# A hybrid conv and S5 layer on one core: the u_s stage by k tiles on unnormalised x, its result laid out anew through memory

## The chip, the cores and the metric

The kernel runs on one core of one Trainium2 chip. The metric is the device time of an execution in microseconds (us). Before the change it is 857.82 us, the median of 3 runs (857.73 to 858.01).

## The reference, cut to what matters

One decoder layer on x of 1024 positions by 1024 channels, all in float32. The input is normalised, projected by one wide matrix, and two mixers run on the projections:

```python
h = rms_norm(x, pre_g)                       # x * rsqrt(mean(x*x) + eps) * gain
proj = h @ w_in
conv_in, z_c, u_s, z_s, g_c, g_s = split(proj)
ca, cb = split(conv_in)
cu = ca * sigmoid(cb)
cu = silu(layer_norm(causal_depthwise_conv(cu, conv_w, conv_b)))     # 31 taps
conv_out = (cu * silu(z_c)) @ w_conv_out
y = gelu(s5_mimo(u_s, ...))                  # 32 groups of 16 channels, 64 complex states each
y = y * sigmoid(y @ w_glu + b_glu)
ssm_out = (y * silu(z_s)) @ w_ssm_out
merged = sigmoid(g_c) * conv_out + sigmoid(g_s) * ssm_out
return x + rms_norm(merged @ w_out, post_g)
```

The reciprocal root mean square of a position, called r below, is one number for each position: it can be multiplied in before a projection or after it. The gain is one number for each input channel.

## The kernel before, in words

**Layout.** The 1024 positions are split as 128 rows n by 8 phases t (position = 8n + t). Products are written with channels on the partitions and positions, ordered by t and then n, on the free axis. To keep float32's accuracy each operand of a matmul is split into a high and a low part (h and l), so every contraction step of 128 costs three passes: h·h, h·l and l·h. A pass of one 128-column output tile over 1024 positions is two matmuls of 512 columns. So one product with eight contraction steps (`product`, L723) has 48 matmuls.

**First stage (L759 to L821).** x comes in eight tiles by phase (`load_x`). `x_front` squares one on ScalarE with a running sum and GpSimd takes the power -1/2 of the mean; `x_mid` multiplies the tile by r and the gain on VectorE; `x_back` transposes it on TensorE in eight blocks, ScalarE copies the high part (`xh`) and VectorE subtracts to get the low part (`xl`). `us_tile` then forms u_s for this phase, 24 matmuls with x as the stationary operand, and ScalarE and VectorE copy the result into four tiles `usb` in which the eight phases of a group lie side by side. Between the passes of phase t the code places the steps of phases t+1 and t+2. The u_s weights have tiles of their own, loaded and split at the start.

**S5.** `s5_params` (L191) makes powers of the eigenvalues from a small table with many short VectorE steps, eight powers on GpSimd (L209) and three sines on ScalarE. Four calls of `s5_quarter` (L354), one for eight groups each, follow. In a quarter VectorE forms `RT`, TensorE transposes it (`rp`) and transposes `usb` (`up`, L389 to L390, 8 blocks) to get U with phase and channel on the partitions; then come the matmuls `ep` (R and U), `kp`, a chain of rotations on VectorE with sines from ScalarE, a scan, a swap of the two halves by DMA (`Zw`), two more steps, the matmuls `yp`, Gelu on ScalarE, and the transposes `yq` back. When all four are done, y is split into `yh` and `yl` (L781 to L785), which the glu products read.

**Conv branch.** `conv_gate` and `conv_taps` (L498, L509) run on VectorE, some 44 steps of 128x512 for each of eight channel tiles; then LayerNorm transposes to positions (`lnp`), takes statistics, normalises, transposes back (`lnq`), ScalarE applies silu, and VectorE multiplies by silu(z_c), read back from memory (L619). `cuh` and `cul`, the split of that, feed the eight `co` products.

**What sets the order.** The order of instructions on each engine is fixed when the program is written: instructions stand in an engine's queue in the order of the code. The products come in the list `seq` (L747 to L757): cb0, ca0, cb1, ca1, gc0 to gc7, two pairs with zc0 between, then the mark "yhl" (S5 must be done), the glu products, and so on, near the end gs6, gs7, the mark "cu", so6, so7 and co0 to co7. S5, conv and LayerNorm are generators that an emission clock (`Clock`, L628) places between the contraction steps. It works in planned units: `tick(dt)` moves the time `now` on by the planned cost of what TensorE was just given; `fg(cost)` adds VectorE work to `dve`, the time at which VectorE is reckoned free; and a generator's next step is written as soon as both its own due time and `dve` are no later than `now`:

```python
for i, t in enumerate(self.tasks):
    if max(t[1], self.dve) <= self.now:
        self.run(i)
        break
```

A step yields its VectorE cost and a delay until the next one. A contraction step of a product counts 1.296. At a mark `until` writes out all that is left of a generator at once. "cu" does so for conv and LayerNorm, "yhl" for S5.

**Buffers.** A pool of 21 tiles of 128x1024 (`T`), two buffers each for raw, high and low weights, and PSUM in two pairs of 128x1024 tiles under the tags "mm" (products) and "aux" (all else). Loads and stores are issued in order on SP; one that waits holds those behind it.

Of the kernel before, what the change touches and what calls it, by code (L numbers as in the profile page):

```python
# [11 lines left out]
ALU = mybir.AluOpType  # L12
# [23 lines left out]
def tile_hybrid_block(  # L36
    ctx: ExitStack,
    tc: tile.TileContext,
    x: bass.AP,
    w_us: bass.AP,  # L40
# [31 lines left out]
    zc_scr = nc.dram_tensor("zc_scratch", (8, 128, 1024), F32, kind="Internal").ap()  # L72
    gc_scr = nc.dram_tensor("gc_scratch", (8, 128, 1024), F32, kind="Internal").ap()
# [20 lines left out]
    iota = const.tile([128, 128], F32, name="iota")  # L94
    lamt = const.tile([128, 3, 32], F32, name="lamt")
# [4 lines left out]
    # ------------------------------------------------------------ loads  # L100
# [3 lines left out]
    xin = {}  # L104
# [5 lines left out]
    preg = T("preg")  # L110
    V.memset(mhalf, -0.5)
    V.memset(halfpi, math.pi / 2)

    # u_s weights, two k-tiles of [128, 512] in one tile
    wus, wusr = {}, {}

    def us_weights(k2):
        wusr[k2] = T(f"wusr{k2}")
        nc.sync.dma_start(out=wusr[k2], in_=w_us[k2])

    def us_split(k2):
        h, l = T(f"wush{k2}", F32R), T(f"wusl{k2}", F32R)
        A.activation(out=h, in_=wusr[k2], func=AF.Copy)
        V.tensor_tensor(out=l, in0=wusr[k2], in1=f32(h), op=ALU.subtract)
        wus[k2] = (h, l)
# [3 lines left out]
    xss = {}  # L129

    def x_front(t):
        xt = xin.pop(t)
        ssq = small.tile([128, 1], F32, tag="ssq", name=f"ssq{t}")
        A.activation(out=xl[:, :, t * 128:(t + 1) * 128], in_=xt.rearrange("p (k n) -> p k n", k=8), func=AF.Square,
                     accum_out=ssq)
        V.tensor_scalar(out=ssq, in0=ssq, scalar1=1.0 / 1024, scalar2=RMS_EPS,
                        op0=ALU.mult, op1=ALU.add)
        r = small.tile([128, 1], F32, tag="rstd", name=f"rstd{t}")
        G.tensor_tensor(out=r, in0=ssq, in1=mhalf[:, 0:1], op=ALU.pow)
        xss[t] = (xt, r)  # L140

    def x_mid(t):
        xt, r = xss[t]
        V.scalar_tensor_tensor(out=xt, in0=xt, scalar=r, in1=preg, op0=ALU.mult, op1=ALU.mult)
        clk.fg(1.2)

    def x_back(t):
        xs, _ = xss.pop(t)
        p = PS(f"xp{t}", "aux")
        for k in range(8):  # L150
            PE.transpose(p[:, k * 128:(k + 1) * 128], xs[:, k * 128:(k + 1) * 128], ident)
        pv = p.rearrange("p (k n) -> p k n", k=8)
        sl = slice(t * 128, (t + 1) * 128)
        A.activation(out=xh[:, :, sl], in_=pv, func=AF.Copy)
        V.tensor_tensor(out=xl[:, :, sl], in0=pv, in1=f32(xh[:, :, sl]), op=ALU.subtract)
        clk.fg(1.2)

    usb = {}

    def us_tile(t):  # L160
        if not usb:
            for c in range(4):
                usb[c] = T(f"usb{c}")
        p = PS(f"usp{t}", "mm")[:, 0:512]
        sl = slice(t * 128, (t + 1) * 128)
        for k in range(8):
            h, l = wus[k // 2]
            kk = slice((k % 2) * 512, (k % 2) * 512 + 512)
            PE.matmul(p, lhsT=xh[:, k, sl], rhs=h[:, kk], start=(k == 0), stop=False)  # L169
            PE.matmul(p, lhsT=xh[:, k, sl], rhs=l[:, kk], start=False, stop=False)  # L170
            PE.matmul(p, lhsT=xl[:, k, sl], rhs=h[:, kk], start=False, stop=(k == 7))  # L171
            if k == 2 and t < 7:
                x_back(t + 1)
            if k == 4 and t + 2 < 8:
                x_front(t + 2)
            if k == 6 and t + 2 < 8:
                x_mid(t + 2)
            clk.tick(0.65)
        for c in range(4):
            src = p[:, c * 128:(c + 1) * 128].rearrange("p (g h) -> p g h", g=8)  # L180
            dst = usb[c].rearrange("p (g j h) -> p g j h", g=8, j=8)[:, :, 7 - t, :]
            if c % 2:
                V.tensor_copy(dst, src)
            else:
                A.activation(out=dst, in_=src, func=AF.Copy)

    # ------------------------------------------------------------ S5
# [166 lines left out]
    def s5_quarter(c, P):  # L354
# [23 lines left out]
        # injection  # L378
# [10 lines left out]
        up = PS(f"up{c}", "aux")  # L389
        pe(lambda g, s: PE.transpose(up[:, s], usb[c][:, s], ident), 0.9)  # L390
# [22 lines left out]
        # rotation tables  # L413
# [80 lines left out]
    # ------------------------------------------------------------ conv branch  # L494
# [132 lines left out]
    # ------------------------------------------------------------ emission clock  # L627
# [41 lines left out]
    # ------------------------------------------------------------ weights  # L669
# [76 lines left out]
    # ------------------------------------------------------------ order of the products  # L746
# [12 lines left out]
    # ------------------------------------------------------------ first part: x and u_s  # L759
    load_x(0)  # L760
    nc.sync.dma_start(out=preg, in_=pre_g.partition_broadcast(128))
    us_weights(0)
    nc.sync.dma_start(out=ident, in_=ident_in)
    us_weights(1)
    load_x(1)
    us_weights(2)
    us_weights(3)
    load_x(2)
    load_x(3)
# [19 lines left out]
    x_front(0)  # L789
    x_mid(0)  # L790
    us_split(0)
    us_split(1)
    x_back(0)
    x_front(1)
    us_split(2)
    x_mid(1)
    us_split(3)
    nc.sync.dma_start(out=iota, in_=iota_in)
# [3 lines left out]
    nc.sync.dma_start(out=bmt, in_=bmat)  # L802
    nc.sync.dma_start(out=chn, in_=chan)
    nc.sync.dma_start(out=cw, in_=conv_w)
    nc.sync.dma_start(out=bgl, in_=bglu)
    clk.now = clk.dve = 0.0
    for t in range(8):
        if t == 1:
            clk.add('s5', s5_chain())
        if t == 3:  # L810
            nc.sync.dma_start(out=cmt, in_=cmat)
            nc.sync.dma_start(out=dmt, in_=dmat)
        if t == 5:
# [126 lines left out]
    # ------------------------------------------------------------ output  # L940
# [67 lines left out]
    for j in range(2):  # L1008
# [78 lines left out]
```

## Time and profile before

| | |
|---|---|
| median of 3 runs | 857.82 us |
| profiled execution, span from first to last instruction | 856.6 us |
| its own time beside the span | not listed; the median is 1.2 us above the span |
| first u_s matmul | at 11.52 us |
| first projection (`pcb`) | at 67.87 us |
| first `co` product | at 675.03 us |
| TensorE (PE) busy | 833.2 us, 97% |
| VectorE (DVE) busy | 593.7 us, 69% |
| ScalarE (ACT) busy | 300.0 us, 35% |
| granted TensorE clock, mean | 0.996 |

How to read the rows below. In a timeline a row gives the start, the duration, the engine (PE matmul, PEld weight load, DVE, ACT, POOL for GpSimd, SPq for a DMA issue), the line of the kernel, the operation, what is written from what, the shape, the count of merged instructions, and in brackets the idle time of the engine ahead of it and what ended it. In the table of stretches a row gives the stretch, its length, the busy times of PE, PEld, DVE, ACT and POOL with instruction counts, the granted clock, the busy share of the DMA engines and GB/s. In the rows of DMA issues the last number is the median time from issue to landing. In the merged chain of work a row gives start, length and what was run.

### The profile page before, as it was taken

How to read it: one execution, taken by the hardware profiler on the slowest of the kernel's cores; microseconds unless marked ns; L12 is line 12 of the kernel's file. 1: busy time of each engine (PE TensorE's matmuls, PEld its weight loads, DVE VectorE, ACT ScalarE, POOL GpSimd, SP SyncE). 2: the span in 40 equal slices, each digit the busy share in tenths (PEclk: the TensorE clock that was granted, in tenths of full speed). 3: DMA queues.
4: the chain of work that ended last, by engine and by line, in shares of the span. 5: the costliest groups of instructions: out<-in, count | busy, mean ns of one | idle time of the engine just before them, and what ended most of it. 6: DMA issues, size and time to landing. Idle time of an engine off the chain costs nothing.

```text
span 856.6 us, 9977 instructions
## 1 busy us (share of the span) xinstructions
PE 833.2 (97%) x3968; PEld 691.3 (81%) x3968; DVE 593.7 (69%) x861; ACT 300.0 (35%) x373; POOL 33.6 (4%) x40
## 2 busy tenths in 40 slices
PE   5999999999999999999999999999999999999996
PEld 4778888888888878888888888788788888888885
DVE  5587898898979999898998999422234744452242
ACT  5333534444435451333322131245644511122121
POOL 0600000000000000000000000010000000000010
PEclk9999999999999999999999999999999999999999
DMA  9202303414323021111121232111216543325142
GB/s 330 104 1 75 84 30 83 138 64 137 99 73 77 26 85 51 50 50 50 37 86 39 74 123 95 54 72 66 72 62 230 221 146 141 143 91 196 50 172 99
DMA packets 28559, 82.93 MB, mean 97 GB/s; under 512 B 7440, under 2 KB 7824, under 8 KB 28512
## 3 DMA queue, kind: packets, MB, share of 16 engines
q1 hardware_dynamic: 28512, 82.29, 28.4%
q8 instruction: 31, 0.51, 0.2%
q14 instruction: 16, 0.13, 0.0%
HBM read 60.13 MB, written 16.78 MB: 90 GB/s over the span
## 4 chain that ended last, share of the span: by engine, by line
PE 92%; DVE 3%; ACT 2%; issue 2%; DMA 1%; SPq 0%; POOL 0%; DVEq 0%; ACTq 0%; POOLq 0%
PE pgc L731 10%; PE pca L731 10%; PE pcb L731 10%; PE pco L731 10%; PE pzc L731 10%; PE po L961 10%; PE pgs L731 9%; PE pzs L731 5%; PE pso L731 5%; PE pgl L731 2%; PE usp L171 1%; PE usp L169 1%; PE usp L170 1%; PE lnq L584 1%; PE yp L482 1%
## 5 line engine op out<-in xcount | busy, mean ns | idle before, releaser
L529 DVE SCALAR_TENSOR_TENSOR pp<-ext,cw,pp 128x512 f32<-128x512 f32 x232 | 165.3, 744 | 1.6 <-ACT pp L520 1.6
L529 DVE SCALAR_TENSOR_TENSOR acc<-ext,hs,acc 128x512 f32<-128x512 f32 x120 | 89.2, 744 | 0.0
L961 PE MATMUL po<-wox,mgh 128*128 128x512 f32 x192 | 52.3, 389 | 0.0
L961 PEld LDWEIGHTS po<-wox,mgh 128*128 128x128 f32 x192 | 36.0, 188 | 7.5
L731 PE MATMUL pzc<-xh,wh_zc 128*128 128x512 f32 x128 | 40.7, 400 | 0.0
L731 PE MATMUL pgc<-xh,wh_gc 128*128 128x512 f32 x128 | 40.3, 396 | 0.0
L731 PE MATMUL pgs<-xh,wh_gs 128*128 128x512 f32 x128 | 40.1, 394 | 0.0
L731 PE MATMUL pca<-xh,wh_ca 128*128 128x512 f32 x128 | 40.0, 394 | 0.0
L731 PE MATMUL pzc<-xl,wh_zc 128*128 128x512 f32 x128 | 40.0, 394 | 0.0
L731 PE MATMUL pcb<-xh,wh_cb 128*128 128x512 f32 x128 | 39.9, 393 | 0.0
L731 PE MATMUL pzc<-xh,wl_zc 128*128 128x512 f32 x128 | 39.8, 393 | 0.0
L731 PE MATMUL pcb<-xh,wl_cb 128*128 128x512 f32 x128 | 39.5, 390 | 0.0
L731 PE MATMUL pgs<-xl,wh_gs 128*128 128x512 f32 x128 | 39.4, 389 | 0.0
L731 PE MATMUL pgc<-xl,wh_gc 128*128 128x512 f32 x128 | 39.4, 389 | 0.0
L731 PE MATMUL pgs<-xh,wl_gs 128*128 128x512 f32 x128 | 39.4, 389 | 0.0
L731 PE MATMUL pco<-cuh,wh_co 128*128 128x512 f32 x128 | 39.4, 389 | 0.0
L731 PE MATMUL pco<-cuh,wl_co 128*128 128x512 f32 x128 | 39.4, 389 | 0.0
L731 PE MATMUL pca<-xl,wh_ca 128*128 128x512 f32 x128 | 39.4, 389 | 0.0
L731 PE MATMUL pgc<-xh,wl_gc 128*128 128x512 f32 x128 | 39.4, 389 | 0.0
L731 PE MATMUL pcb<-xl,wh_cb 128*128 128x512 f32 x128 | 39.4, 389 | 0.0
L731 PE MATMUL pca<-xh,wl_ca 128*128 128x512 f32 x128 | 39.4, 389 | 0.0
L731 PE MATMUL pco<-cul,wh_co 128*128 128x512 f32 x128 | 39.4, 389 | 0.0
(260 smaller groups left out, 1765.6 us busy)
## 6 DMA issues: line engine op xcount, KB each, us to landing
xin<-in_x_dram SPq DMA_DIRECT2D x8, 512.0 KB, 4.7
wr_cb<-in_w_in_dram SPq DMA_DIRECT2D x8, 512.0 KB, 3.3
wr_ca<-in_w_in_dram SPq DMA_DIRECT2D x8, 512.0 KB, 3.2
wr_gc<-in_w_in_dram SPq DMA_DIRECT2D x8, 512.0 KB, 3.4
gc_scratch<-gct SPq DMA_DIRECT2D x8, 512.0 KB, 2.8
wr_zc<-in_w_in_dram SPq DMA_DIRECT2D x8, 512.0 KB, 3.3
zc_scratch<-zct SPq DMA_DIRECT2D x8, 512.0 KB, 2.6
wr_gs<-in_w_in_dram SPq DMA_DIRECT2D x8, 512.0 KB, 3.2
```

The source lines that it names most:

```text
L169: PE.matmul(p, lhsT=xh[:, k, sl], rhs=h[:, kk], start=(k == 0), stop=False)
L170: PE.matmul(p, lhsT=xh[:, k, sl], rhs=l[:, kk], start=False, stop=False)
L171: PE.matmul(p, lhsT=xl[:, k, sl], rhs=h[:, kk], start=False, stop=(k == 7))
L482: PE.matmul(yp[:, s], lhsT=Sx[:, s], rhs=O1[:, s], start=False, stop=True)
L529: V.scalar_tensor_tensor(out=o, in0=src(e, r), scalar=w, in1=o, op0=ALU.mult, op1=ALU.add)
L584: PE.transpose(q[:, s], tn[:, s], ident)
L731: PE.matmul(p[:, js(j)], lhsT=lhs[:, ks], rhs=rhs(k, j), start=st, stop=sp_)
L961: PE.matmul(p[:, js(j)], lhsT=lhs[k][:, s], rhs=rhs[k][:, js(j)], start=st, stop=sp_)
```

## The change

x is also given transposed, as `xt` of eight tiles by channel (128 channels by 1024 positions in the order t, n). The first stage no longer waits for r: it runs over the eight contraction tiles k, with all four u_s output tiles accumulating in the eight PSUM banks ("aux" and "mm" both), weights as the stationary operand. x is scaled by the gain alone and split (`x_raw`). The squares still come from x by phase; when all eight are done, r is formed at once for all (`x_rstd`), written to memory as 8 by 128, and read back as one row on all partitions (`rbc`). The u_s results are multiplied by it as they leave PSUM (`us_out`), stored to `us_scr`, and read back in eight pieces, one for each phase, directly as U. The transposes `up` of the S5 quarters and the tiles `usb` go. The projections after the stage still need normalised x, so `x_norm` multiplies each raw tile by gain and r and splits it again into `xh` and `xl`. The u_s weights now share the two raw, high and low weight buffers. `seq` and the generators' costs stay, but for the clock calls of the new stage and the `up` group's 0.9.

```diff
+    us_scr = nc.dram_tensor("us_scratch", (4, 128, 1024), F32, kind="Internal").ap()
+    r_scr = nc.dram_tensor("r_scratch", (8, 128), F32, kind="Internal").ap()
...
+    def us_split(k2, part, parts):
...
+        A.activation(out=h[:, s], in_=wusr[k2][:, s], func=AF.Copy)
+        V.tensor_tensor(out=l[:, s], in0=wusr[k2][:, s], in1=f32(h[:, s]), op=ALU.subtract)
+        clk.fg(1.15 / parts)
...
+    def x_raw(k):
+        A.activation(out=xh[:, k, :], in_=xraw[k], func=AF.Copy, scale=gcol[:, k:k + 1])
+        V.scalar_tensor_tensor(out=xl[:, k, :], in0=xraw[k], scalar=gcol[:, k:k + 1], in1=f32(xh[:, k, :]),
+                               op0=ALU.mult, op1=ALU.subtract)
+        clk.fg(1.28)
+
+    def x_square(t):
+        xi = xin.pop(t)
+        A.activation(out=xi, in_=xi, func=AF.Square, accum_out=ssq8[:, t:t + 1])
+
+    def x_rstd():
+        V.tensor_scalar(out=ssq8, in0=ssq8, scalar1=1.0 / 1024, scalar2=RMS_EPS, op0=ALU.mult, op1=ALU.add)
+        G.tensor_tensor(out=r8t, in0=ssq8, in1=mhalf, op=ALU.pow)
+        nc.sync.dma_start(out=r_scr.rearrange("t n -> n t"), in_=r8t)
+        rbc = T("rbc")
+        nc.sync.dma_start(out=rbc, in_=r_scr.rearrange("t n -> (t n)").partition_broadcast(128))
+        return rbc
+
+    def x_norm(k, rbc):
+        xn = xraw.pop(k)
+        V.scalar_tensor_tensor(out=xn, in0=xn, scalar=gcol[:, k:k + 1], in1=rbc, op0=ALU.mult, op1=ALU.mult)
+        A.activation(out=xh[:, k, :], in_=xn, func=AF.Copy)
+        V.tensor_tensor(out=xl[:, k, :], in0=xn, in1=f32(xh[:, k, :]), op=ALU.subtract)
+        clk.fg(2.5)
...
+    def us_out(m, p, rbc):
+        u = T(f"usT{m}")
+        V.tensor_tensor(out=u, in0=p, in1=rbc, op=ALU.mult)
         clk.fg(1.2)
+        nc.sync.dma_start(out=us_scr[m], in_=u)
+        usU[m] = T(f"U{m}")
+        src = us_scr[m].rearrange("(g h) (t n) -> t h g n", g=8, t=8)
+        for t in range(8):
+            nc.sync.dma_start(out=usU[m][16 * (7 - t):16 * (8 - t)].rearrange("p (g n) -> p g n", g=8), in_=src[t])
...
-        up = PS(f"up{c}", "aux")
-        pe(lambda g, s: PE.transpose(up[:, s], usb[c][:, s], ident), 0.9)
...
-        U = T(f"U{c}")
-        A.activation(out=U, in_=up, func=AF.Copy)
+        U = usU[c]
...
+    load_xt(0)
+    nc.sync.dma_start(out=gcol, in_=pre_g)
+    us_weights(0, 2)
+    load_xt(1)
     load_x(0)
...
+    usp = {m: PS(f"usp{m}", "aux" if m < 2 else "mm") for m in (0, 1, 2, 3)}
+    for k in range(2):
+        x_raw(k)
+        us_split(0, k, 2)
+    rbc = None
+    for k in range(8):
...
+        if k + 2 < 8:
+            x_raw(k + 2)
+            if k % 2 == 0:
+                us_split(k // 2 + 1, 0, 1)
+        for t in {0: (0,), 1: (1, 2), 2: (3, 4), 3: (5, 6), 4: (7,)}.get(k, ()):
+            x_square(t)
+        if k == 4:
+            rbc = x_rstd()
             for _ in range(WRAW):
                 wload()
...
+        ms = (2, 3, 0, 1)
+        runs = [(m, i) for m in ms for i in range(3)] if k == 7 else [(m, i) for i in range(3) for m in ms]
+        for n_, (m, i) in enumerate(runs):
...
+            if n_ == 5:
+                for k_ in {5: (0, 1, 2), 6: (3, 4), 7: (5,)}.get(k, ()):
+                    x_norm(k_, rbc)
+            if k == 6 and n_ == 8:
+                wsplit_h()
+                wsplit_l()
+            clk.tick(0.45)
+            if k == 7 and i == 2:
+                if m == 0:
+                    x_norm(6, rbc)
+                us_out(m, usp[m], rbc)
+    x_norm(7, rbc)
```

In the loop the S5 generator is added at k = 1 (at t = 1 before). The loads of x, xt, the u_s weights and the small tables are issued in a new order, among and ahead of these steps.

More of the change, by code (lines that the diff above doesn't have):

```diff
@@ L39, in tile_hybrid_block @@
     x: bass.AP,
+    xt: bass.AP,
     w_us: bass.AP,
@@ L102, in tile_hybrid_block @@
     ov = out.rearrange("(n t) d -> t n d", t=8)
-    xin = {}
+    V.memset(mhalf, -0.5)
+    V.memset(halfpi, math.pi / 2)
+    xin, xraw = {}, {}
     def load_x(t):
@@ L108, in load_x, with load_xt, us_weights @@
         nc.sync.dma_start(out=xin[t], in_=xv[t])
-    preg = T("preg")
-    V.memset(mhalf, -0.5)
-    V.memset(halfpi, math.pi / 2)
+    def load_xt(k):
+        xraw[k] = T(f"xt{k}")
+        nc.sync.dma_start(out=xraw[k], in_=xt[k])
     wus, wusr = {}, {}
[L117 to L125, printed above, removed]
+    def us_weights(k2, parts=1):
+        wusr[k2] = wp.tile([128, 1024], F32, tag="wraw", name=f"wusr{k2}", bufs=WRAW)
+        n = 1024 // parts
+        for i in range(parts):
+            nc.sync.dma_start(out=wusr[k2][:, i * n:(i + 1) * n], in_=w_us[k2][:, i * n:(i + 1) * n])
@@ new lines, in us_split @@
+    def us_split(k2, part, parts):
+        if part == 0:
+            wus[k2] = (wp.tile([128, 1024], F32R, tag="wh", name=f"wush{k2}", bufs=WHL),
+                       wp.tile([128, 1024], F32R, tag="wl", name=f"wusl{k2}", bufs=WHL))
+        h, l = wus[k2]
+        n = 1024 // parts
+        s = slice(part * n, (part + 1) * n)
+        A.activation(out=h[:, s], in_=wusr[k2][:, s], func=AF.Copy)
+        V.tensor_tensor(out=l[:, s], in0=wusr[k2][:, s], in1=f32(h[:, s]), op=ALU.subtract)
+        clk.fg(1.15 / parts)
@@ L142, in x_mid @@
-    def x_mid(t):
-        xt, r = xss[t]
-        V.scalar_tensor_tensor(out=xt, in0=xt, scalar=r, in1=preg, op0=ALU.mult, op1=ALU.mult)
-        clk.fg(1.2)
[L147 to L185, printed above, removed]
+    ssq8 = const.tile([128, 8], F32, name="ssq8")
@@ L757, in tile_hybrid_block @@
     order += [u for u in seq if u[0] not in NOW] + [("wo", k) for k in range(WHL)]
+    load_xt(0)
+    nc.sync.dma_start(out=gcol, in_=pre_g)
+    us_weights(0, 2)
+    load_xt(1)
     load_x(0)
-    nc.sync.dma_start(out=preg, in_=pre_g.partition_broadcast(128))
-    us_weights(0)
-    nc.sync.dma_start(out=ident, in_=ident_in)
+    load_xt(2)
     us_weights(1)
[L765 to L769, printed above, removed]
     nc.sync.dma_start(out=lamt, in_=lam)
     nc.sync.dma_start(out=cst, in_=cst_in)
+    load_x(1)
+    load_x(2)
+    load_xt(3)
+    load_x(3)
+    load_xt(4)
     P5 = {}
@@ new lines, in tile_hybrid_block @@
+    for k in range(2):
[3 more added lines that the diff above has]
+    for k in range(8):
+        if k == 0:
+            load_x(4)
+            us_weights(2)
+            load_x(5)
+            load_x(6)
+            load_xt(5)
+            load_x(7)
+            nc.sync.dma_start(out=bmt, in_=bmat)
+        if k == 1:
+            clk.add('s5', s5_chain())
+            nc.sync.dma_start(out=chn, in_=chan)
+            nc.sync.dma_start(out=cw, in_=conv_w)
+            load_xt(6)
+        if k == 2:
+            us_weights(3)
+            load_xt(7)
+            for d_, s_ in ((iota, iota_in), (ident, ident_in), (bgl, bglu), (cmt, cmat), (dmt, dmat)):
+                nc.sync.dma_start(out=d_, in_=s_)
+        if k + 2 < 8:
[6 more added lines that the diff above has]
+            rbc = x_rstd()
@@ new lines, in tile_hybrid_block @@
+        for n_, (m, i) in enumerate(runs):
+            lhs, rhs = passes[i]
+            for j in range(2):
+                js_ = slice(j * 512, (j + 1) * 512)
+                PE.matmul(usp[m][:, js_], lhsT=lhs[:, kk[m]], rhs=rhs[:, k, js_], start=(k == 0 and i == 0),
+                          stop=(k == 7 and i == 2))
+            if n_ == 5:
[9 more added lines that the diff above has]
+                us_out(m, usp[m], rbc)
```

49 lines of the change are left out of this document (10 added, 39 removed).

## The prediction

> **What bounds the kernel now.** I read the page first: the span, the engines, the chain of work that ended last.
>
> ```profile
> span 856.6 us, 9977 instructions
> PE 833.2 (97%) x3968; PEld 691.3 (81%) x3968; DVE 593.7 (69%) x861; ACT 300.0 (35%) x373; POOL 33.6 (4%) x40
> PE 92%; DVE 3%; ACT 2%; issue 2%; DMA 1%; SPq 0%; POOL 0%; DVEq 0%; ACTq 0%; POOLq 0%
> ```
>
> TensorE is the bound. Next the busy times by stretch, cut at the first projection (67.87), the first glu product (294.06) and the first co product (675.03).
>
> ```profile
> 67.87:294.06 226.19, 226.19 (x1234) 191.73 (x1233) 199.24 (x270) 100.49 (x101) 3.82 (x4) 1.00 0.29 84
> 294.06:675.03 380.97, 376.85 (x1713) 311.08 (x1712) 277.06 (x402) 138.43 (x185) 7.85 (x8) 1.00 0.22 77
> 675.03:856.60 181.57, 174.54 (x769) 143.93 (x767) 73.16 (x71) 32.59 (x42) 4.40 (x8) 0.99 0.39 139
> ```
>
> Per stretch: length, then PE, PEld, DVE, ACT, POOL. From 67.87 to 675.03 TensorE idles 0.00 + 4.12 us: every chain on VectorE ends just in time, by an order of instructions that is fixed in advance. VectorE is busy 88% of the first stretch. So two questions decide: does the first projection start sooner than 67.87, and do the chains still end in time? What lies after 675.03 is the same work in both; I keep its 181.6.
>
> **The first stage, TensorE's side.** The timeline and the merged chain:
>
> ```profile
> 4.21 1.06 ACT L134 ACTIVATE xl<-xin 128x1024 fp32r<-128x1024 f32 x1 [2.20 <-DMA xin<-in_x_dram]
> ...
> 11.52 0.80 PE L169 MATMUL usp<-wush,xh 128*128 128x512 f32 x1 [1.36 <-ACT xh L154]
> ...
> 14.03 0.63 PE L170 MATMUL usp<-wusl,xh 128*128 128x512 f32 x1
> ...
> 14.45 0.63 PE L171 MATMUL usp<-wush,xl 128*128 128x512 f32 x1
> ...
> 75.71 0.87 PE up L390 x8
> ...
> 95.62 10.88 PE pcb L731 x48
> ```
>
> Warm, a 512-column matmul takes a slot of 10.88/48 = 0.227 us; early on the slot is 0.42 (14.03 to 14.45). The first raw transposed tile should land as the first x tile does (4.2); scaling it (1.06), half a weight split and the gain's small load put the first matmul at about 6.5 instead of 11.5. The 192 matmuls take 43.5, slow slots at first add some 2: u_s ends near 52. If that were all, the first projection would start 16 us sooner. The four `up` groups, 0.87 each, go as well: **-3.5**.
>
> **The first stage, VectorE's side.** The projections need normalised x, and it comes from one queue: eight x_norm, each a VectorE multiply, a ScalarE copy that VectorE waits for, and a VectorE subtract, with the us_out between them. The steps, from equal operations:
>
> ```profile
> 6.62 1.28 DVE L144 SCALAR_TENSOR_TENSOR xin<-xin,rstd,preg 128x1024 f32<-128x1024 f32 x1 [1.07 <-DMA preg<-in_pre_g_dram]
> ...
> 7.91 1.06 ACT L123 ACTIVATE wush<-wusr 128x1024 fp32r<-128x1024 f32 x1 [2.55 <-DMA wusr<-in_w_us_dram]
> ...
> 9.00 1.23 DVE L124 TENSOR_TENSOR wusl<-wusr,wush 128x1024 fp32r<-128x1024 f32 x1 [1.09 <-ACT wush L123]
> ...
> 22.86 3.26 POOL L209 TENSOR_TENSOR spt<-ebase,lamt 128x8 f32<-128x8 f32 x2 [2.28 <-DVE ebase L203]
> 38.88 0.18 DVE L212 SCALAR_TENSOR_TENSOR spt<-spt,spt 128x32 f32<-128x32 f32 x1
> ...
> 41.04 0.19 DVE L199 TENSOR_TENSOR turns<-turns,spt 128x32 f32<-128x32 f32 x1
> 0.00:22.00 22.00, 12.16 (x46) 9.41 (x46) 11.40 (x15) 10.84 (x14) 1.86 (x7) 1.00 0.90 332
> preg<-in_pre_g_dram SPq DMA_DIRECT2D x1, 512.0 KB, 5.3
> bgl<-in_bglu_dram SPq DMA_DIRECT2D x1, 2.0 KB, 3.7
> wr_cb<-in_w_in_dram SPq DMA_DIRECT2D x8, 512.0 KB, 3.3
> gc_scratch<-gct SPq DMA_DIRECT2D x8, 512.0 KB, 2.8
> ```
>
> One x_norm is 1.28 + 1.09 + 1.23 = 3.6, since nothing stands between its two VectorE steps; a us_out or a weight's subtract is 1.2. When can the first begin? It needs all eight squares, the power, r to memory and back.
>
> The loads do not set this: at 332 GB/s (row of 0 to 22) the 10.6 MB up to the last u_s weight land by 32. What does is the S5 parameters' order on VectorE. Raw tile 3 is the ninth 512 KB: 4.7 MB at 332 is 14, its copy and subtract end at 17.4, and only then comes the memset that S5's first powers wait for. Four powers of 1.63 on GpSimd (3.26 for two) end at 24, 0.7 of VectorE, four more at 31.4. The steps on theta stand in VectorE's queue ahead of raw tile 6, and there it waits: 2.7 for them (the same steps ran from 38.9 to 41.2), tile 6 and weight split 3 (2.5), the small step: 36.8. A power on 128x8 is 1.64: 38.5.
>
> The round trip of r is not in the trace. Its store is 1,024 pieces of 4 bytes. From below it is a 2 KB load (3.7 beside other loads; without them perhaps 2.4) and a plain 512 KB load (3.3), so 5.7; from above I double the first and take the broadcast row, 7.4 + 5.3 = 12.7. I take 3.7 + 5.3 = 9.0, the rows of like shape. So the row of r is there at **47.5** (44 to 51).
>
> The Trainium skill, "DMA: Bandwidth & Descriptors", "Rules for kernel authors", speaks against this store: a strided last dimension becomes one descriptor per element. No run here shows its price; by that page's fit for the GpSimd path (2.0 us plus bytes/436 GB/s, "Anatomy of one DMA") an estimate for both trips is 5.2, and the sum below would be 3.8 less.
>
> From 47.5, in VectorE's order: x_norm 0 to 4 (18.0), cb0's weight subtract, us_out 2, which frees the PSUM pair that cb0 writes: 47.5 + 18.0 + 2.4 = 67.9. **cb0 starts where it starts now**, after TensorE has idled some 16 us. Then x_norm 5, us_out 3, x_norm 6, us_out 0 and 1, x_norm 7: 10.8 + 3.6 = 14.4, to 82.3. cb0's last contraction step, due 9.5 after its start, at 77.4, needs that: **+4.9** (+1.5 to +8.5).
>
> SP's queue: each us_out is a store (2.8 and its issue) and eight loads that wait for it, issued at about 0.6 as the eight `Mt` copies are (254.93, in the next fence: 5.24 for x8): 8 us, four times, from 67.9 to 100. Behind them is the load of ca1's weights, landing at 103, split at 105.5, when ca1 begins (83.7 + 2 x 10.9): 0 (to +6). U of quarter 0, third in that order, lands near 94; its first reader stands at 112.
>
> **The order written ahead.** Products and VectorE tasks are placed by the emission clock; I followed its costs through both listings. Before: the stage ends at 41.6 of the clock, VectorE reckoned free at 39.9. After: 96 ticks of 0.45 are 43.2, but 8 x 2.5 + 4 x 1.2 + 1.14 from 29.3 on make VectorE free at 55.2. So the rest of S5's parameters waits, and quarter 0 starts 26 units into the projections instead of 1. Before, S5's last step comes at 257.06 and the place where glu needs it ("yhl") at 257.06: no slack. After, "yhl" stands at 250.7, with quarter 3's kp product emitted at 239.8, seven contraction steps earlier. All that is left of S5 is then put there in one piece, with no product between. The trace has each step:
>
> ```profile
> 249.33 0.21 PE L424 MATMUL kp<-O,bb 128*16 128x16 f32 x2
> ...
> 252.41 0.28 DVE L438 TENSOR_TENSOR kr<-kp,dmt 16x128 f32<-16x128 f32 x1 [4.34 <-ACT kr L437]
> ...
> 254.93 5.24 SPq L445 DMA_DIRECT2D Mt<-kr  x8
> ...
> 256.74 0.74 DVE L529 SCALAR_TENSOR_TENSOR pp<-ext,cw,pp 128x512 f32<-128x512 f32 x1
> ...
> 257.40 0.74 DVE L529 SCALAR_TENSOR_TENSOR acc<-ext,hs,acc 128x512 f32<-128x512 f32 x1
> ...
> 268.01 2.63 DVE L463 TENSOR_TENSOR_SCAN Zs<-r,Et 128x128 f32<-128x128 f32 x8
> ...
> 275.44 1.23 DVE L371 TENSOR_TENSOR Zw<-Zw,tk 128x1024 f32<-128x1024 f32 x1 [0.89 <-DMA Zw<-Zs]
> ...
> 285.23 1.28 ACT L486 ACT_TABLE_LOAD   x1 [5.31 <-PE yp L482]
> ...
> 286.52 1.03 ACT L486 ACTIVATE yt<-yp 128x1024 f32<-128x1024 f32 x1
> ...
> 289.09 1.03 PE L489 MATMUL yq<-ident,yt 128*128 128x128 f32 x8
> ...
> 292.21 4.63 DVE L784 TENSOR_TENSOR yl<-y,yh 128x1024 fp32r<-128x1024 f32 x4 [1.41 <-ACT yh L783]
> ```
>
> From kp's start: kr at 3.1, its 0.28 and five S5 steps (0.7 + 4 x 1.2), six conv taps (0.66 each) and one half weight (0.7) queued between: 13.4; the add 1.2; scan to 17.1; half swap (270.64 to 275.44) to 21.9; two more steps: 24.4. TensorE is there after 1.8 + 7 x 1.36 = 11.4: it waits 13.0 for yp. Then yp 3.5, Gelu and its table load 2.5, yq, and from yq's start 7.75 until the fourth split (289.09 to 296.84): glu's last step at 38.2, its end at 39.1, against 21.2 without waits: **+17.8** (+14 to +20).
>
> LayerNorm likewise. The last conv channel ends at 519.4 of the clock instead of 495.5, "cu" stands at 599.4 (603.2). Before, all eight rounds and all multiplies by z were placed by 603.2; after, round 8 and the eight multiplies fall behind "cu", with only so6 and so7 as cover.
>
> ```profile
> 545.84 1.03 PE L559 MATMUL lnp<-ident,acc 128*128 128x128 f32 x8
> ...
> 551.73 1.09 PE L584 MATMUL lnq<-ident,tn 128*128 128x128 f32 x8 [2.12 <-ACT tn L575]
> ...
> 645.41 2.90 ACT L588 ACTIVATE acc<-lnq,chn 128x128 f32<-128x128 f32 x8
> ...
> 650.43 2.35 DVE L619 TENSOR_TENSOR acc<-acc,zcr 128x1024 f32<-128x1024 f32 x2
> ...
> 666.00 1.23 DVE L619 TENSOR_TENSOR acc<-acc,zcr 128x1024 f32<-128x1024 f32 x1 [2.09 <-DMA zcr<-zc_scratch]
> ```
>
> lnp to lnq is 5.9 here, with a first power of 1.5; 5.1 with the usual 0.55, less 0.8 of its own: 4.3. From lnq: silu 1.3 to 4.2, eight multiplies 9.8 if back to back, 16.8 as they run now (650.43 to 667.2, waiting for loads); I take 12.8: 17. so7's weights are subtracted behind them (0.7), while so7 wants its third pass at 0.8 + 5.5 + 0.9 = 7.2: 10.5. Together **+14.8** (+11 to +19). co0 finds its splits in time. Of the 4.1 idle now, lnq0's 2.1 stays: **-2.0**.
>
> After long idle TensorE is slow, as at the start: 3.2 us at 0.42 are 7.5 matmuls, 0.2 each, 1.5. At "yhl" and "cu" together **+3.0**; from below 0, if a wait inside the kernel leaves no trace, from above 4. The Trainium skill, "TensorE: Matmul & The Clock Gate", Part 1, says that the array falls to half its clock after an idle window of about 3.4 us. The slow slots at 14 agree with that, though the granted clock reads 1.00 in that stretch; no long idle time later on is in this trace to show it.
>
> Sum: -3.5 + 4.9 + 0 + 17.8 + 14.8 - 2.0 + 3.0 = **+35.0**. Span 891.6. The median, 857.82, is 1.2 above the profiled span: **893**.
>
> **The rivals.** *The clock's lag is not real and the row of r is early* (chance 0.08): if x_norm keeps up with TensorE the projections start at 52 and S5 has time; 857.8 - 16 - 3.5 = 838. For it: VectorE has 12% to spare. Against: it decides only if the row of r is there by 52 - 20.4 = 32, and the queue gives 38.5 before the round trip. *Only the first stage counts* (0.04): +4.9 - 3.5, 859; it needs "yhl" and "cu" covered, and no product stands there. *Half cover* (0.12): r early and the multiplies back to back, with one of the waits at "yhl" or "cu" gone: 893 - 16 = 877. *SP's queue decides* (0.10): the 32 U loads keep weights from ScalarE through several products, as ScalarE stands still behind each; twice 6 us: 905. Forecast: 0.66.
>
> **How the numbers follow.** All lows of the terms give 878, all highs 911; both at once are unlikely. With the half-cover case below and the queue's above the range is 874 to 906; it leaves out the first two rivals and the forecast's own tails, some 2 in 10. A difference under 0.2% (1.7 us) I call the same: the runs shown spread 0.3 us. Faster: 0.08. Same: most of the 859 case, 0.03. Slower: the rest, 0.89.
>
> **What would show it.** Right: TensorE idle from about 52 to 68, waiting for us_out 2; x_norm steps 3.6 apart, the first waiting for rbc's load; a wait of 13 before yp in the last quarter, right ahead of glu; a wait at the last lnq and one in so7. Wrong: cb0 starting by 60, an uninterrupted TensorE around glu, or the eighth lnp well ahead of so6.

## The result and the profile after

The changed kernel takes **948.0 us** (median of 4 runs, 947.43 to 949.99) against 857.81 us (4 runs, 857.73 to 858.01): a ratio of 1.1057, 95% interval 1.1041 to 1.1073. It is slower, as forecast, but by 90 us instead of 35, and outside the range. The page of the changed kernel (profiled in the run of 949.99), its span and the busy times of the engines:

```profile
span 948.0 us, 9816 instructions
PE 843.0 (89%) x3872; PEld 696.2 (73%) x3872; DVE 605.3 (64%) x851; ACT 304.1 (32%) x364; POOL 28.8 (3%) x33
```

TensorE had 97% and has 89%: it waits. VectorE's busy time grew by 11.6 us only, so the change does not cost work, it costs waiting. The table of stretches of the changed kernel, cut where the prediction cut it: at the first projection (74.75), the first glu product (323.06) and the first `co` product (766.55). Columns: length, then busy times of PE, PEld, DVE, ACT, POOL, then granted clock, DMA share, GB/s.

```profile
74.75:323.06 248.31, 230.66 (x1201) 193.34 (x1201) 209.36 (x300) 96.39 (x95) 3.82 (x4) 0.96 0.32 93
323.06:766.55 443.49, 392.39 (x1713) 321.77 (x1713) 287.42 (x414) 144.41 (x190) 5.94 (x8) 0.93 0.20 69
766.55:948.00 181.45, 174.54 (x769) 143.88 (x767) 72.78 (x71) 32.30 (x41) 4.32 (x8) 0.99 0.38 133
```

The last stretch is what it was (181.45 against 181.57). The first projection comes 6.9 later, the next stretch is 22 longer, and the one from glu to `co` is 62.5 longer: the larger part of the loss lies nearly 300 us behind the edited stage, at the waits from 380 on. Which waits? The table of TensorE's waits (sum, times, longest), cut:

```profile
PE pcb L724 <- DVE usT L175: 22.0, 1, 22.0
PE pso L724 <- ACT wh_so L691: 19.9, 2, 10.6
PE pzs L724 <- ACT wh_zs L691: 16.0, 2, 9.7
PE yp L475 <- DVE Sx L468: 12.2, 1, 12.2
PE lnq L577 <- ACT tn L568: 8.1, 4, 4.0
...
PE pso L724 <- DVE wl_so L699: 6.5, 1, 6.5
...
```

The rows for `usT`, `Sx`, `tn` and the `wl_so` row are the prediction's own waits. The rows for `wh_so` and `wh_zs`, 35.9 us in four waits, stand nowhere in it. The timeline around the first of these four, in the changed kernel:

```profile
360.42 1.23 DVE L699 TENSOR_TENSOR wl_zs<-wr_zs,wh_zs 128x1024 fp32r<-128x1024 f32 x1 [5.40 <-ACT wh_zs L691]
361.56 0.75 DVE L522 SCALAR_TENSOR_TENSOR pp<-ext,cw,pp 128x512 f32<-128x512 f32 x1
...
381.64 0.68 DVE L532 TENSOR_TENSOR acc<-acc,pp 128x512 f32<-128x512 f32 x1
...
382.28 1.18 DVE L494 TENSOR_TENSOR ext<-pca,sg 128x1024 f32<-128x1024 f32 x1
383.50 0.71 DVE L497 TENSOR_TENSOR ext<-ext 128x528 f32<-128x528 f32 x1
384.24 1.19 ACT L498 ACTIVATE ext<-ext 128x1179 f32<-128x1179 f32 x1 [23.85 <-DVE ext L497]
385.33 1.04 ACT L691 ACTIVATE wh_zs<-wr_zs 128x1024 fp32r<-128x1024 f32 x1
...
386.43 1.22 PE L724 MATMUL pzs<-xh,wh_zs 128*128 128x512 f32 x2 [6.28 <-ACT wh_zs L691]
```

Read it upwards from the last row. TensorE waits for a high weight half on ScalarE. That copy takes 1.04 and its data is there, but ScalarE, which works in order, has stood for 23.85 behind the gate's copy into `ext` (L498). That copy waits for the gate on VectorE, and the gate stands behind the whole rest of the last convolution channel, 361.56 to 382.3, without a break. This is the line `clk.until('conv', lambda: conv_left[0] < n)`: if two channels are pending when a gate comes, the rest of one is written ahead of it in one piece. The emission clock does this at gates 4, 5, 6 and 7 after the change, with 15 to 20 of its units in each piece, and at none before. In the trace ScalarE stands behind these four gates for 23.9, 27.3, 27.4 and 28.6 us.

How long each stretch has become, in the changed kernel (start and end, then length): the two pairs of `zs`, the first `gs` with its `so`, `gs` 1 with `so` 1, the last S5 quarter with glu, and the stretch at cu.

```profile
369.10:398.97 29.87, 23.59 (x97) 19.05 (x96) 19.88 (x29) 6.45 (x6) 0.00 (x0) 0.89 0.10 36
420.73:455.42 34.69, 24.94 (x98) 20.04 (x96) 23.29 (x34) 6.44 (x6) 0.00 (x0) 0.80 0.09 31
477.18:505.38 28.20, 18.81 (x74) 15.06 (x72) 20.46 (x32) 3.82 (x5) 0.00 (x0) 0.82 0.12 38
527.14:556.56 29.42, 18.86 (x74) 15.06 (x72) 21.63 (x34) 3.82 (x5) 0.00 (x0) 0.83 0.09 27
299.92:347.34 47.42, 31.44 (x137) 26.29 (x136) 22.33 (x29) 14.56 (x16) 0.00 (x0) 0.82 0.14 41
737.42:766.55 29.13, 18.67 (x66) 14.85 (x64) 19.71 (x21) 17.45 (x25) 0.54 (x1) 0.71 0.52 184
```

Without waits a projection takes 10.88 and an `so`, or a glu product, half of that. So the first four cost 29.87 - 21.76 = 8.1, 12.9, 28.20 - 16.32 = 11.9 and 13.1: **46.0** together. The fifth holds yp, yq and four glu products, 3.5 + 0.85 + 21.76 = 26.1 without waits: **+21.3**. The sixth holds `so` 6, `so` 7 and one lnp and lnq, 12.6: **+16.5**. At the start cb0 ends at 90.33 instead of 78.75: **+11.6**. With the four `up` groups gone (-3.5) the sum is 91.9; `co` 0 starts 91.5 later. Not all of this is waiting: in these rows TensorE is also busy longer than the work takes, by 10.0 at the four gates together, 5.3 in the fifth and 6.1 in the sixth. That is the slow clock after a wait, shown in the last section.

The first stage of the changed kernel, its timeline:

```profile
37.65 1.64 POOL L158 TENSOR_TENSOR r8t<-ssq,mhalf 128x8 f32<-128x8 f32 x1 [4.88 <-DVE spt L229]
39.31 0.40 SPq L159 DMA_DIRECT2D r_scratch<-r8t  x1
48.33 0.34 SPq L161 DMA_DIRECT2D rbc<-r_scratch  x1
54.48 1.28 DVE L166 SCALAR_TENSOR_TENSOR xt<-xt,gcol,rbc 128x1024 f32<-128x1024 f32 x1 [11.33 <-DMA rbc<-r_scratch]
...
74.75 1.19 PE L724 MATMUL pcb<-xh,wh_cb 128*128 128x512 f32 x2 [22.02 <-DVE usT L175]
```

The load of r's row waits for its store, issued 9.0 earlier; from the store's issue to the first x_norm pass 15.2.

### The profile page after: what moved, and what is told of

Same layout as the page of the kernel before. It is cut to its first block, busy times and chain, and to the rows that moved or that the text cites. A ratio compares the mean times of both kernels' runs of the same rounds, so it can differ in the third digit from the quotient of the medians.

```text
span 948.0 us, 9816 instructions
## 1 busy us (share of the span) xinstructions
PE 843.0 (89%) x3872; PEld 696.2 (73%) x3872; DVE 605.3 (64%) x851; ACT 304.1 (32%) x364; POOL 28.8 (3%) x33
## 2 busy tenths in 40 slices
DMA packets 36221, 91.31 MB, mean 96 GB/s; under 512 B 9344, under 2 KB 13824, under 8 KB 36176
## 3 DMA queue, kind: packets, MB, share of 16 engines
q1 hardware_dynamic: 36176, 90.69, 28.6%
## 4 chain that ended last, share of the span: by engine, by line
PE 58%; DVE 24%; ACT 5%; DMA 5%; issue 5%; POOL 2%; SPq 1%; DVEq 0%; POOLq 0%; ACTq 0%
PE pzc L724 9%; PE pco L724 9%; PE po L985 9%; DVE pp L522 8%; PE pcb L724 6%; PE pgs L724 5%; PE pso L724 5%; DVE acc L522 4%; PE pca L724 3%; PE pzs L724 3%; PE pgl L724 2%; PE pgc L724 2%; DMA xt<-in_xt_dram 1%; POOL spt L205 1%; DMA Zw<-Zs 1%
## 5 line engine op out<-in xcount | busy, mean ns | idle before, releaser
L522 DVE SCALAR_TENSOR_TENSOR pp<-ext,cw,pp 128x512 f32<-128x512 f32 x232 | 164.6, 744 | 12.7 <-ACT pp L513 12.7
L498 ACT ACTIVATE ext<-ext 128x1179 f32<-128x1179 f32 x8 | 9.5, 1186 | 138.3 <-DVE ext L497 138.3
L724 PEld LDWEIGHTS pcb<-xh,wh_cb 128*128 128x128 f32 x128 | 24.1, 192 | 28.7 <-issue 22.6
L724 PE MATMUL pso<-y2h,wh_so 128*128 128x512 f32 x64 | 24.0, 461 | 19.9 <-ACT wh_so L691 19.9
```

The costliest lines, as they stand in the source:

```text
L498: A.activation(out=ext[:, :, 0:3, 1:132], in_=ext[:, :, 4:7, 0:131], func=AF.Copy)
L522: V.scalar_tensor_tensor(out=o, in0=src(e, r), scalar=w, in1=o, op0=ALU.mult, op1=ALU.add)
L724: PE.matmul(p[:, js(j)], lhsT=lhs[:, ks], rhs=rhs(k, j), start=st, stop=sp_)
```

## The experiments

The theory: the loss is in the order that the emission clock writes. Its lag makes it put pieces ahead of gates, of yp and behind cu, and the engines that work in order then hold weights back. The main rival: VectorE really has too little time, wherever the pieces stand. A separate question is r's round trip. Each experiment is one run, only the last has six; the kernel before took 856.3 to 858.7 us beside them. The six runs of the last version spread over 2.9 us, so a smaller difference between single runs isn't read as a gain.

**The clock set back at the end of the stage.** Only the written order of what follows differs.

```diff
     P5_ready[0] = True
+    clk.dve = clk.now
```

> The new kernel with one line more: at the end of the first stage the emission clock's reckoning of VectorE is set back to its present time (55.2 to 43.2). No work is added or removed, only the places of later instructions move. Theory (written order: S5 and conv are placed too late against the products, and what is left at the marks and ahead of gates 4 to 7 is written in one piece that holds back the next weights): the four pieces ahead of the gates shrink from 15 to 20 units to 5 to 10, so the four waits (46 us over the matmuls' own time with the slow slots after them) fall to 10 to 15, the one at glu (21) to about 10, the end (16.5) to about 11; 890 to 905. Rival (the new stage's extra VectorE work, its memory traffic and SP's queue are the cost): 944 to 950, as the work is the same.

Measured: 919.87. The gain, 28, is outside both bands. TensorE's waits in this run:

```profile
PE pca L724 <- DVE wl_ca L699: 8.3, 2, 7.5
...
PE pso L724 <- ACT wh_so L691: 4.8, 2, 2.6
PE yp L475 <- DVE Sx L468: 4.6, 1, 4.6
PE pzs L724 <- ACT wh_zs L691: 2.8, 1, 2.8
```

The gates' waits fall from 35.9 to 7.6 and yp's from 12.2 to 4.6, with VectorE's work unchanged. But the clock now calls VectorE free when it isn't: the rest of the S5 parameters is written ahead of ca0's low half, and TensorE waits 7.5 there. The wait in `so` 7 stayed at 6.5. The order is the cause, but pretending that the lag is gone is no cure.

**r stored as 128 by 8**, and read by VectorE in steps of 32 bytes.

```diff
-        nc.sync.dma_start(out=r_scr.rearrange("t n -> n t"), in_=r8t)
+        nc.sync.dma_start(out=r_scr, in_=r8t)
...
+        return rbc.rearrange("p (n t) -> p t n", t=8)
```

> The new kernel, but r goes to memory as 128 rows of 8 (128 pieces of 32 bytes, as it lies) instead of 8 rows of 128 (1,024 pieces of 4 bytes); the broadcast row is then read by VectorE with a stride of 8. Theory (the many small pieces of the store are the dear half of r's round trip of 15 us): the store lands in 2.5 to 3.5 instead of 8.6, the first x_norm starts at 48 to 49 instead of 54.5, the first projection near 69 instead of 74.75, and the time falls by 5 to 6: 942. Rival (what costs is the two trips' fixed latency, not the pieces): the store still takes over 6, 946 to 949. If the strided read slows VectorE, x_norm's first step shows it (1.28 now).

Measured: 947.58. The timeline of this run:

```profile
38.66 0.35 SPq L159 DMA_DIRECT2D r_scratch<-r8t  x1
40.10 0.33 SPq L161 DMA_DIRECT2D rbc<-r_scratch  x1
44.25 2.18 DVE L167 SCALAR_TENSOR_TENSOR xt<-xt,gcol,rbc 128x1024 f32<-128x1024 f32 x1 [1.75 <-DMA rbc<-r_scratch]
```

The store lets the load go after 1.4 instead of 9.0, and the first x_norm runs 10.2 earlier. But every x_norm multiply, which reads the row, takes 2.05 to 2.20 instead of 1.28, and VectorE's queue gives the gain back: cb0 starts at 69.42, 5.3 earlier, then waits 5.8 for the last x_norm and ends at 90.49 (90.33 in the change). The time alone would have said that the store doesn't matter; the trace says that it does and that the edit paid for it elsewhere.

**A row of ones instead of r**: no store, no load, and so no normalisation of x.

```diff
-        nc.sync.dma_start(out=r_scr.rearrange("t n -> n t"), in_=r8t)
         rbc = T("rbc")
-        nc.sync.dma_start(out=rbc, in_=r_scr.rearrange("t n -> (t n)").partition_broadcast(128))
+        G.memset(rbc, 1.0)
```

> The new kernel without r's trip through memory: the row that x_norm and us_out multiply by is filled with ones on GpSimd, so the normalisation is left out and nothing waits for the squares. Theory (r's round trip is what x_norm waits for, all of it on the path to the first projection): x_norm starts when VectorE has finished raw tile 7, near 43.5, the first projection stands near 64 instead of 74.75, and the total falls by 10 to 11: 937. Rival (the stage is bound by VectorE's own queue or by TensorE): the first projection moves by less than 4, 944 or more.

Measured: 937.01, as the theory had it. TensorE's wait at cb0:

```profile
PE pcb L723 <- DVE usT L174: 10.0, 1, 10.0
```

It is 12 shorter (22.0), the time 11; the waits at the gates, at yp and in `so` 7 are the same to 0.1. So the whole round trip is worth 11 us of the 90, and an earlier start moves nothing of the rest: there the order decides.

**The gate's copy on GpSimd** instead of ScalarE, so that ScalarE no longer stands behind the gate.

```diff
-        A.activation(out=ext[:, :, 0:3, 1:132], in_=ext[:, :, 4:7, 0:131], func=AF.Copy)
+        G.tensor_copy(ext[:, :, 0:3, 1:132], ext[:, :, 4:7, 0:131])
```

> The new kernel, with the copy at the end of each conv gate on GpSimd instead of ScalarE, so that ScalarE's queue doesn't stand behind VectorE there. Theory (VectorE's own piece ahead of the gate holds the low half of the next weights as well, which stands behind the gate in its queue): each of the four waits shrinks by 1 to 3 only, 936 to 946. Rival (it is ScalarE's standing, with the high halves behind it, that stops TensorE): the four waits go, and with them 36 to 46: 902 to 912.

Measured: 937.56. TensorE's waits in this run:

```profile
PE pso L724 <- DVE wl_so L699: 19.8, 3, 7.9
...
PE pzs L724 <- DVE wl_zs L699: 9.3, 2, 6.3
```

The waits for high halves are gone, and waits for low halves stand in their place: VectorE's own queue has the piece ahead of those too. (The longest of the first row, 7.9, is `so` 7's. At the four gates 21.2 are left for low halves and 5.4 for PSUM tiles that ScalarE empties, of 35.9.) ScalarE's standing behind the gate was the last wait to end, and worth about 10 us; the piece on VectorE is the cause.

**The order alone.** The first stage stays as in the change. First LayerNorm's delays, then the place of three products, then both (with one product more moved, ahead of cb6 and ca6).

```diff
-        yield 0.0, 3.0
+        yield 0.0, 2.0
...
-        yield 1.4, 2.2
+        yield 1.4, 2.0
...
-        yield 0.1, 5.4
+        yield 0.1, 3.0
```

> Edit: the changed kernel with LayerNorm's three delays on the emission clock alone made shorter (3.0, 2.2, 5.4 become 2.0, 2.0, 3.0); the list of products is as in the change. On the clock the multiplies by z then end 2 behind cu instead of 25 behind it. Theory (the excess at cu, 16.5, comes from where those steps are written): the waits at the last lnq and in so7 go, those at the gates and at yp stay as they are: 931 to 936. Rival (VectorE reaches these steps late whatever their place): above 943.

Measured: 935.60. The waits at the gates and at yp are 19.9, 16.0 and 12.2 as before; the wait in `so` 7 is gone, and the longest at lnq is 2.8. Of the 16.5 at cu, some 12 went by three numbers of the clock.

```diff
-    seq = pairs[0] + pairs[1] + gc + pairs[2] + zc[0:1] + pairs[3] + [("yhl", 0)] + glu + pairs[4] + zs[0:2]
+    seq = pairs[0] + pairs[1] + gc + pairs[2] + zc[0:1] + pairs[3] + zc[1:4] + [("yhl", 0)] + glu + pairs[4] + zs[0:2]
-    seq += pairs[5] + zs[2:4] + pairs[6] + [("y2", 0)] + gso[0] + pairs[7] + gso[1] + gso[2] + zc[1:8]
+    seq += pairs[5] + zs[2:4] + pairs[6] + [("y2", 0)] + gso[0] + pairs[7] + gso[1] + gso[2] + zc[4:8]
```

> Edit: the changed kernel with three zc products alone moved ahead of glu; LayerNorm's delays are as in the change. On the clock no piece stands ahead of gates 4 to 7, nothing is left of S5 at yhl, and the multiplies by z end 15 behind cu instead of 25. Theory (46.0 at the gates and 21.3 at yp come from the place of these products): both go but for a few us, and of the 16.5 at cu some 7 to 12 stay: 881 to 892. Rival (the moved products bring the waits of the gates back at other places): above 900.

Measured: 877.26, better than the band by 4. TensorE's waits behind cb0 are these and two of 0.7 and 0.2:

```profile
PE lnq L577 <- ACT tn L568: 6.8, 3, 2.8
PE pso L724 <- DVE wl_so L699: 4.7, 1, 4.7
PE pgl L724 <- DVE wl_glu L699: 1.8, 1, 1.8
```

No wait at a gate or at yp is left, and `so` 7's is shorter: 70.7 us from the place of three products, with no work added or removed.

> Edit: the first stage as in the changed kernel; only the list of products is other (three zc products stand ahead of glu, one ahead of the sixth pair) and LayerNorm's three delays on the emission clock are shorter (3.0, 2.2, 5.4 become 2.0, 2.0, 3.0). By the clock's arithmetic no piece is then put ahead of a gate, before yp or behind cu without cover. Theory (46.0 at the gates, 21.3 at yp and 16.5 at the last lnq and so7 come from the written order alone): the first projection starts as before at 74.8, those waits shrink to some 2 to 3 each, and the time is 866 to 885. Rival (VectorE's work does not fit behind the products since it begins them later, wherever the pieces are put): the waits come back elsewhere and the time stays above 915.

Measured: 870.71. The table of stretches of this run, from its first projection to glu and from glu to `co`:

```profile
74.79:337.08 262.29, 260.01 (x1344) 217.69 (x1345) 232.83 (x330) 108.12 (x106) 3.83 (x4) 0.99 0.33 97
337.08:687.03 349.95, 343.76 (x1570) 284.34 (x1569) 263.54 (x385) 129.02 (x176) 6.48 (x8) 1.00 0.22 76
```

The first projection comes where it came, at 74.8; behind it TensorE idles 2.3 + 6.2 us instead of 17.7 + 51.1. VectorE's busy time in the two, 496.4, is what it was (209.36 + 287.42 = 496.8). The rival is refuted: VectorE had time enough for the same work.

**The start of the projections.** Both edits build on r stored as 128 by 8. First ScalarE brings the row into the order of t once, so that VectorE's steps are contiguous again; then VectorE issues the next multiply ahead of the last low half.

```diff
+        rb = T("rb")
+        A.activation(out=rb.rearrange("p (t n) -> p t n", t=8), in_=rbc.rearrange("p (n t) -> p t n", t=8), func=AF.Copy)
+        return rb
...
```

> Edit: r is stored as 128 pieces of 32 bytes, and ScalarE brings the broadcast row into the order of t once (1.1 us), so that VectorE reads it contiguously again. Theory (the round trip of r delays the start of the projections one for one, and nothing behind it gives the time back): the first x_norm at about 46 instead of 54.5, the first projection about 20.3 behind it at 66 instead of 74.8, the time some 8.5 below the changed kernel: 938 to 941. Rival (VectorE's lag at the waits further on decides, wherever the projections start): 945 to 949.

Measured: 945.16, a miss, and by the time alone the rival's. The trace shows that the step expected, an earlier x_norm, did not come about. The timeline of this run:

```profile
44.34 2.15 ACT L163 ACTIVATE rb<-rbc 128x1024 f32<-128x1024 f32 x1 [10.31 <-DMA rbc<-r_scratch]
...
48.40 1.13 ACT L147 ACTIVATE xh<-xt,gcol 128x1024 fp32r<-128x1024 f32 x1
49.57 1.28 DVE L148 SCALAR_TENSOR_TENSOR xl<-xt,gcol,xh 128x1024 fp32r<-128x1024 f32 x1 [10.18 <-ACT xh L147]
```

The copy stands in ScalarE's queue ahead of raw tile 7, so ScalarE waits 10.3 for the row, tile 7 is late, and VectorE's queue has tile 7's low half ahead of the first x_norm, which runs at 52.0 and not at 46.

```diff
+        xnq.append((k, xn))
+        if len(xnq) > 1:
+            x_low()
...
```

> Edit: the one before, and VectorE issues the multiply of the next x_norm before the low part of the last one, so that it doesn't stand waiting for ScalarE's copy. Theory: x_norm about 2.5 apart instead of 3.6; five of them stand ahead of the first projection, so it starts some 5.5 sooner, near 61; the waits at the gates, at yp and in so7 stay, since their order is the same: 930 to 936. Rival (ScalarE's copy becomes the step that sets the pace): no more than 2 below the run before.

Measured: 938.23, outside the band, since the run that it builds on was 4 us worse than expected; the step itself brought 6.9. x_norm runs 2.3 apart instead of 3.55.

**Both together**, then two repairs of the stage: the copy of the row behind raw tile 7, and r formed earlier.

> Edit: the runs with the pipelined x_norm and with the other order together. Theory (the start of the projections and the order add up): 14 below the run with the other order alone, 850 to 870, and near 852 if its waits are as small as the clock says, which is below the kernel before. Rival (with TensorE waiting less, another engine's chain ends last, so that the two don't add): less than 6 below the run with the other order alone.

Measured: 862.04, inside the band, but 8.7 below the run with the other order alone and not 14. The same edits of the start had brought 9.8 without the other order (948.0 to 938.23): but for 1.1 they add up, and the start itself is worth less than expected, since the copy is misplaced.

```diff
-        rb = T("rb")
-        A.activation(out=rb.rearrange("p (t n) -> p t n", t=8), in_=rbc.rearrange("p (n t) -> p t n", t=8), func=AF.Copy)
...
+            if n_ == 5 and k == 5:
+                rbc = x_row(rbc)
```

> Edit: the run with both, and ScalarE's copy of the row of r stands behind the high half of raw tile 7 instead of ahead of it, where it held that tile back. Theory: the first x_norm at about 47 instead of 52.4, and the first projection as much earlier, near 61: the time about 5.5 lower, 855 to 858. Rival (u_s itself, which ends near 54, and the x_norm behind it leave the start where it is): less than 2 lower.

Measured: 854.49, 7.6 less and just below the band; the first projection starts at 60.64, as expected.

```diff
+            load_x(7)
             load_xt(5)
-            load_x(7)
...
-        for t in {0: (0,), 1: (1, 2), 2: (3, 4), 3: (5, 6), 4: (7,)}.get(k, ()):
+        for t in {0: (0,), 1: (1, 2), 2: (3, 4), 3: (5, 6, 7)}.get(k, ()):
             x_square(t)
-        if k == 4:
+        if k == 3:
             rbc = x_rstd()
```

> Edit: the one before, and x's eighth tile is loaded and squared earlier, so that the small step and the power of r stand ahead of the last two powers of the S5 parameters on GpSimd and of theta on VectorE. Theory: r is stored near 31 instead of 39, its row is there near 37, the first x_norm runs near 40 to 42 and the first projection starts at 55 to 57, a few us behind the end of u_s: 849 to 853, below the kernel before (857.8). Rival (the S5 parameters, pushed back, come late instead, and VectorE's queue holds the start where it was): 855 to 858, no gain over the run before this one.

Measured: **853.01 us** (6 runs, 851.58 to 854.49) against 857.80, a ratio of 0.9949, 95% interval 0.9935 to 0.9962. This version is 0.5% below the kernel before, a small gain but clear of the noise; against the run before it, 854.49, no gain is shown. Its timeline:

```profile
32.45 0.35 SPq L159 DMA_DIRECT2D r_scratch<-r8t  x1
...
41.60 0.23 ACT L275 ACTIVATE sn<-phi 128x32 f32<-128x32 f32 x1 [7.78 <-DVE phi L208]
...
42.21 1.14 ACT L147 ACTIVATE xh<-xt,gcol 128x1024 fp32r<-128x1024 f32 x1
43.25 2.19 ACT L166 ACTIVATE rb<-rbc 128x1024 f32<-128x1024 f32 x1
...
59.97 1.19 PE L737 MATMUL pcb<-xh,wh_cb 128*128 128x512 f32 x2 [6.89 <-DVE usT L188]
```

r is stored 6.3 earlier, and yet the projections start only 0.7 earlier than in the run before, later than the 55 to 57 expected: the S5 parameters, pushed back, now hold ScalarE's queue: its Sin steps wait 7.8 for VectorE's `phi` and stand ahead of tile 7 and of the row's copy. That is the rival's mechanism, on ScalarE's queue as well as VectorE's. TensorE still waits 6.9 at cb0.

## Why the prediction was wrong

The direction was right, and so were most mechanisms in the sum; the size was not, since a place was missing. Every sign that the prediction named for being right came, and they could not show the missing place. Point by point:

| term | predicted | measured |
|---|---|---|
| `up` groups gone | -3.5 | not separable, -3.5 kept |
| first stage, to the end of cb0 | +4.9 | +11.6 |
| SP's queue | 0 | no wait seen for it |
| last quarter and glu ("yhl"), slow clock included | +17.8 + 1.5 | +21.3 |
| last LayerNorm and so7 ("cu"), slow clock included | +14.8 + 1.5 | +16.5 |
| waits at lnq that would go | -2.0 | 0: 4.1 ahead of the last, 3.6 before the change |
| gates 4 to 7 | not in the sum | **+46.0** |

**The step that failed is "The order written ahead".** It followed the emission clock through both listings for S5 and LayerNorm, and found the two places named. It left out the third consumer of the same lag, the `until` ahead of a gate; the price of such a piece, some 20 to 30 taps of 0.66, could be had from the rows that it quoted for the conv. The bound "all highs give 911" was a bound over the terms listed, not over the places where the lag can come out. The moved products show the cause: with three of them elsewhere the gates' waits and yp's are gone, and the delays alone remove most of cu's.

**The round trip of r** was mis-sized: 9.0 predicted, with 12.7 as its upper end, and 15.2 measured. The store alone holds the load back 9.0, where the prediction took 3.7, a 2 KB load; the broadcast row took 6.1, close to the 5.3 taken. The small step, the power (37.65 for 36.8), x_norm's spacing (3.55 for 3.6) and the order up to cb0 came as worked out. cb0 itself took 4.7 longer than 10.88, close to the 4.9 predicted, but by luck: it waited only 1.5 for x_norm 7, and the rest is the slow clock after its waits. The Trainium skill, "DMA: Bandwidth & Descriptors", "Rules for kernel authors", warns of just this store, one descriptor per element. Its fit gave an estimate of 5.2 for both trips; with 128 pieces of 32 bytes they took 5.6, with 1,024 pieces of 4 bytes 15.2. The trace agrees with the rule: the page of the changed kernel counts 9,344 packets under 512 bytes, that of the run with 128 pieces 8,449, so 895 fewer where 1,024 less 128 is 896. The fit came near for the 128 pieces and was about three times too low for the 1,024.

**Yhl and cu** were right in place and mechanism: yp waited 12.2 (13.0 predicted), the last lnq and `so` 7 waited 4.0 and 6.5 (4.3 and 10.5 predicted). That their totals came so close is in part luck, since two errors cancel. TensorE's idle time in the two rows was 16.0 and 10.5, where 17.8 and 14.8 were predicted, and the slow clock cost 5.3 and 6.1, where the prediction took 1.5 for each.

Of the rivals, none held. "SP's queue decides" was the dearest, at 905, but no wait of TensorE for a load stands behind the start; "the clock's lag is not real" is refuted in its strong form, since the lag put 83.8 us into the time.

## What to carry to other kernels

Where an order is written ahead by a model's clock, a change that shifts the clock must be followed to every place that reads it, and the price of each forced piece counted on the engines that stand in line behind it: the loss can lie hundreds of us behind the edit and be several times what the edited stage itself loses (here 83.8 beside 11.6). When waits appear far from an edit, move independent work between the pieces before touching the edit. And look at what a faster step stands behind in its own engine's queue: three of the repairs here (the clock set back, the row's copy, the early r) gave back part of their gain to an instruction that was merely ahead of it in order.

## What the runs showed of the hardware

**Small pieces.** A store of 4 KB in 1,024 pieces held the load behind it back 9.0 us from its issue, in 128 pieces 1.4, and 2.2 in the last version.

**A strided operand.** A scalar_tensor_tensor of 128 by 1,024 takes 1.28 on VectorE, 2.05 to 2.20 when one input is read in steps of 32 bytes; ScalarE's copy with such an input took 2.15 to 2.19 and a contiguous one 1.06.

**The clock after idle time** shows in the granted clock, and much less idle time than expected brings it about. The table of stretches of the changed kernel, right behind the waits of 22.02 and 6.28, the second also a little later:

```profile
74.75:79.00 4.25, 4.25 (x10) 3.38 (x11) 3.13 (x3) 1.06 (x1) 0.00 (x0) 0.50 0.62 236
386.43:390.00 3.57, 3.57 (x9) 2.85 (x10) 2.42 (x2) 2.27 (x2) 0.00 (x0) 0.54 0.35 119
390.00:394.00 4.00, 4.00 (x20) 3.26 (x19) 2.36 (x2) 2.01 (x2) 0.00 (x0) 1.00 0.06 25
```

And of the run with the other order, behind a wait of 2.82 and behind one of 1.76:

```profile
607.70:611.00 3.30, 3.30 (x14) 2.66 (x13) 0.00 (x0) 3.29 (x9) 0.00 (x0) 0.56 0.03 5
345.40:348.00 2.60, 2.60 (x12) 2.14 (x13) 2.60 (x5) 1.86 (x3) 0.00 (x0) 1.00 0.28 101
```

For 3 to 4 us the clock is about half. At the four gates this cost 1.8 to 3.2 us each: TensorE was busy 23.59, 24.94, 18.81 and 18.86 us with work of 21.76, 21.76, 16.32 and 16.32. So of the gates' 46.0 the waits make 35.9 and the slow clock some 10. The Trainium skill, "TensorE: Matmul & The Clock Gate", Part 1, puts the idle window at about 3.4 us; here 2.82 was enough. The prediction said that the trace of before has no such case later on. It has one, at the lnq of 551.73 whose wait of 2.12 it quoted; the table of stretches of the kernel before shows a clock of 0.67 there:

```profile
551.70:555.00 3.30, 3.27 (x14) 2.78 (x15) 0.00 (x0) 2.14 (x7) 0.00 (x0) 0.67 0.22 83
```

The length of one wait does not decide alone. The single wait of 1.76 left the clock at 1.00, but in the changed kernel two short ones close together, 0.98 and 0.53 at the end of cb0 (before 87.57 and 88.83), were followed by 0.62:

```profile
88.50:92.00 3.50, 3.17 (x8) 2.48 (x9) 3.29 (x12) 2.70 (x3) 0.00 (x0) 0.62 0.70 225
```

What rule of idle time fits all these cases, the runs do not show. What made the prediction's slots at the kernel's start slow (0.42) while the granted clock read 1.00 there stays open.
